# Router weights as the stationary operand, and both parts of the GLU's input as one moving operand

## The chip, the cores and the metric

The kernel runs on one core of a Trainium2 chip. A core has TensorE (matrix products into PSUM, a small accumulator memory of eight banks), VectorE, ScalarE, GpSimd and SyncE, which issues the loads. The metric is the time of the program on the device in microseconds, the median of several runs.

## The reference

One decoder layer on 256 tokens of width 2048, all in float32. What matters here:

```python
# state-space branch, u: (256, 1024)
z = gelu(y)
out = z * sigmoid(z @ w_glu)               # w_glu: 1024 x 1024, "the GLU"
merged = sigmoid(gate_ssm) * (out @ w_branch_ssm) + sigmoid(gate_att) * (y_att @ w_branch_att)
x = x + merged @ w_out
# experts
h2 = rms_norm(x, ffn_norm_g)
g_logits = h2 @ router_group_w + router_group_b      # 4 groups
e_logits = h2 @ router_expert_w + router_expert_b    # 32 experts
# top group, top 2 of its 8 experts, gates; then for every expert e
x = x + combine[:, e] * ((silu(h2 @ w_gate[e]) * (h2 @ w_up[e])) @ w_down[e])
```

The 36 router columns (4 + 32) are one weight matrix of 2048 x 36 in the kernel.

## The kernel before

The first phase is a list of blocks of dense products, worked off in steps; each step takes a slab of 256 x 512 weights. A slab is loaded into `raw` five steps ahead and split two steps ahead into a high part `wh` (ScalarE) and a low part `wl` (VectorE) in a rounded float32 form that TensorE multiplies in one pass. The activations are kept as high and low parts too, and a product is the sum of three: high by high, low by high, high by low. Most blocks (`b_orient`) use the activations as the stationary operand and 512 weight columns as the moving one, with two PSUM tiles. The two GLU blocks (`a_orient`) use the weights as the stationary operand and 256 tokens of z as the moving one, with four PSUM tiles `acc` (there are four such banks, handed out in turn). `glu_fin` empties them: ScalarE takes the sigmoid out of PSUM, VectorE multiplies by z, and after all four ScalarE and VectorE split the result into `ys`, the input of the next block (`wbs`).

The last block is `wout`, in four quarters n. After each, x is transposed (`x2_tr`) and `route_mm` adds its share to the router's logits: the transposed x (128 x 128) is the stationary operand and 36 router columns the moving one, plain float32, which TensorE takes as two instructions per product. So there are four visits of 16 instructions. The last quarter's follow when the products are over. Then TensorE does 36 transposes without use (`keep_busy(WARM[0])`) while VectorE works out the norm `rs2`, adds the bias and selects group and experts (`first_max`, tiles R). A product with a triangular matrix (`ult`) gives each token its rank, and expert 0 begins: `gather` picks tokens, `gate_up` multiplies by the weights, four column groups at a time (`tile_position`).

In the second phase the weights of 32 experts stream through a ring of 11 buffers (10 later) of 2 MB, six pieces an expert; `load_piece` issues a piece's load when a buffer's products have been issued, and the load waits on the last of them. The first 7 pieces are loaded ahead, during the blocks before, the others as memory of the first phase comes free.

Every engine works off its instructions in the order in which the program writes them (a manual schedule); a helper records most of them, so that the profile shows line 77 for all.

Of the kernel before, what the change touches and what calls it, by code (L numbers as in the profile page):

```python
# [9 lines left out]
F32 = mybir.dt.float32  # L10
F32R = mybir.dt.float32r
I32 = mybir.dt.int32
AF = mybir.ActivationFunctionType
OP = mybir.AluOpType
# [3 lines left out]
P = 128  # L18
T = 256
# [63 lines left out]
def hybrid_block(ctx, tc, A, out):  # L83
    nc = tc.nc
    load = {"vec": 0.0, "act": 0.0, "pe": 0.0}
    vec = Meter(nc.vector, load, "vec")
    act = Meter(nc.scalar, load, "act")
    pe = Meter(nc.tensor, load, "pe")
    sp, pool = nc.sync, nc.gpsimd
# [3 lines left out]
    def unit(i, shape, dt, name):  # L93
        return U[i].tile(shape, dt, name=name, tag="u")
# [4 lines left out]
    cp = ctx.enter_context(tc.tile_pool(name="cp", bufs=1))  # L99
    wctx = ExitStack()  # L100
    cq = wctx.enter_context(tc.tile_pool(name="cq", bufs=1))
# [6 lines left out]
    def acc_tile(name="acc"):  # L108
        return pacc.tile([P, 512], F32, name=name, tag="acc")

    def bg_tile(k):
        return pbg.tile([P, 512], F32, name="bg" + "ab"[k], tag="bg" + "ab"[k])
# [4 lines left out]
    def add_block(src, nk, begin, mm, fin):  # L117
        blocks.append((src, nk, begin, mm, fin))
# [12 lines left out]
    def split(i):  # L131
        if i >= len(subs):
# [12 lines left out]
    g1 = cq.tile([P, 16], F32, name="g1")  # L145

    small = cq.tile([P, 3, 32], F32, name="lamdt")
    cq.tile([P, 88], F32, name="level")
    dsk = cq.tile([P, 16], F32, name="dsk")
    qkg = cq.tile([P, 2], F32, name="qkg")  # L150
    g2 = cp.tile([P, 16], F32, name="g2")
    wrg = cq.tile([P, 16, 36], F32, name="wrg")
    rbias = cp.tile([P, 36], F32, name="rbias")
# [9 lines left out]
                       base=0, channel_multiplier=1)  # L163
    ult = cp.tile([P, P], F32, name="ult")
    pool.affine_select(out=ult, in_=ones, pattern=[[1, P]], compare_op=OP.is_gt, fill=0.0,
                       base=0, channel_multiplier=-1)
# [3 lines left out]
                       base=0, channel_multiplier=-1)  # L170
    dmask = cq.tile([P, 32], F32, name="dmask")
    pool.memset(dmask, 0.0)
    for i in range(4):
        pool.affine_select(out=dmask, in_=dmask, pattern=[[-1, 32]], compare_op=OP.not_equal, fill=1.0,
                           base=-32 * i, channel_multiplier=1)
# [22 lines left out]
    uT = uy[:, 0]  # L198
# [21 lines left out]

        add_block(src, nk, begin, mm, lambda: fin(st["a"]))

    def a_orient(src, nk, rh, rl, fin, banks, flag=None):
        st = {}

        def begin():
            if flag:
                need(flag)
            st["a"] = banks()

        def mm(s, h, l):
            for x, w in ((rh, h), (rl, h), (rh, l)):
                for kk in range(2):
                    k = 2 * s + kk
                    for m in range(4):
                        pe.matmul(st["a"][m][:, 0:T], w[:, kk, m * P:m * P + P], x(k),
                                  start=(k == 0 and w is h and x is rh), stop=(k == nk - 1 and w is l))

        add_block(src, nk, begin, mm, lambda: fin(st["a"]))

    acc4 = lambda: [acc_tile() for _ in range(4)]
# [27 lines left out]
    S = {}  # L269
# [47 lines left out]
    def glu_fin(n):  # L317
        def f(a):
            if n == 0:
                ys = unit(7, [P, 2, 8, T], F32R, "ys")  # L320
                S["ys"] = (ys[:, 0], ys[:, 1])
            for m in range(4):
                b = 4 * n + m
                act.activation(uT[:, b], a[m][:, 0:T], AF.Sigmoid)
                vec.tensor_tensor(uT[:, b], uT[:, b], yT[:, b], op=OP.mult)
            for m in range(0, 4, 2):
                b = slice(4 * n + m, 4 * n + m + 2)
                act.copy(S["ys"][0][:, b], uT[:, b])
                vec.tensor_tensor(S["ys"][1][:, b], uT[:, b], S["ys"][0][:, b], op=OP.subtract)
        return f  # L330

    for n in range(2):
        a_orient(A["wglu"][n], 8, lambda k: S["z"][0][:, k], lambda k: S["z"][1][:, k], glu_fin(n), acc4, "z")

    def ssm_fin(n):
        def f(a):
# [25 lines left out]
        b_orient(A["wbs"][n], 8, lambda k: S["ys"][0][:, k], lambda k: S["ys"][1][:, k], ssm_fin(n))  # L362

    ssq = cp.tile([P, 2, 4], F32, name="ssq")
    def out_fin(n):
        def f(a):
            c = slice(512 * n, 512 * n + 512)
            x2 = S["x2"]
            if n == 0:
                S["xt2"] = {}  # L370
                S["lg"] = [bg_tile(1), bg_tile(1)]
            for t in range(2):
                vec.tensor_tensor(x2[:, t, c], x2[:, t, c], a[t], op=OP.add)
            for t in range(2):
                later(D_X2 if n < 3 else 1, lambda t=t: x2_tr(n, t))
            for t in range(2):
                later(D_ROUTE if n < 3 else 2, lambda t=t: route_mm(n, t))
        return f

    def x2_tr(n, t):  # L380
        ps = bg_tile(0)
        for i in range(4):
            k = 4 * n + i
            pe.transpose(ps[:, P * i:P * i + P], S["x2"][:, t, P * k:P * k + P], ident)
        xt = S["xt2"][n, t] = slot((2 * n + t) % 4, [P, 4, P], F32, "xt2")
        act.copy(xt, ps.rearrange("p (i c) -> p i c", i=4))
        junk = slot(4 + (2 * n + t) % 4, [P, 512], F32, "junk")
        xs = S["x2"][:, t, 512 * n:512 * n + 512]
        if n < 3:
            act.activation(junk, xs, AF.Square, accum_out=ssq[:, t, n:n + 1])  # L390
            if n == 2 and t == 1:
                act.activation(tiny, ones[:, 0:1], AF.Sqrt)
        else:
            vec.scalar_tensor_tensor(junk, xs, 1.0, xs, op0=OP.mult, op1=OP.mult, accum_out=ssq[:, t, n:n + 1])

    def route_mm(n, t):
        for i in range(4):
            k = 4 * n + i
            pe.matmul(S["lg"][t][:, 0:36], S["xt2"][n, t][:, i], wrg[:, k], start=(k == 0), stop=(k == 15))

    for n in range(4):
        b_orient(A["wout"][n], 16, lambda k: S["m"][k // 8][:, 0, k % 8], lambda k: S["m"][k // 8][:, 1, k % 8], out_fin(n))
# [4 lines left out]
    for b, s in turns:  # L407
        src, nk, begin, mm, fin = blocks[b]
# [318 lines left out]
    def gelu():  # L727
        while "scan" not in prog:
            yield 0
        while "att" not in prog:  # L730
            yield 0
        zz = unit(9, [P, 2, 8, T], F32R, "zz")
        S["z"] = (zz[:, 0], zz[:, 1])
        c0 = math.sqrt(2.0 / math.pi) * 0.044715
        stage = [0] * 4
        while min(stage) < 5:
            for p in range(4):
                y, w = yT[:, 2 * p:2 * p + 2], uT[:, 2 * p:2 * p + 2]
                k = stage[p]
                if k > 4 or ("y", 2 * p + 1) not in prog:  # L740
                    continue
                if k == 0:
                    act.activation(w, y, AF.Square)
                elif k == 1:
                    vec.scalar_tensor_tensor(w, w, 1.0 / 0.044715, y, op0=OP.add, op1=OP.mult)
                elif k == 2:
                    act.activation(w, w, AF.Tanh, scale=c0)
                    vec.tensor_scalar(y, y, 0.5, None, op0=OP.mult)
                elif k == 3:
                    vec.scalar_tensor_tensor(y, w, 1.0, y, op0=OP.add, op1=OP.mult)  # L750
                    act.copy(S["z"][0][:, 2 * p:2 * p + 2], y)
                else:
                    vec.tensor_tensor(S["z"][1][:, 2 * p:2 * p + 2], y, S["z"][0][:, 2 * p:2 * p + 2], op=OP.subtract)
                stage[p] += 1
            yield 0
        prog["z"] = True
# [125 lines left out]
    def later(d, f):  # L882
        pend.append((prog["step"] + d, f))
# [9 lines left out]
    def need(flag):  # L893
        while flag not in prog:
            assert gens
            for g in list(gens):
                if next(g, None) is None:
                    gens.remove(g)
# [8 lines left out]
    for i in range(nsub):  # L907
        prog["step"] = i
        src, s, nk, begin, mm, fin = subs[i]
# [8 lines left out]
        h, l = hl_t.pop(i)  # L918
# [35 lines left out]
    rt = ctx.enter_context(tc.tile_pool(name="rt", bufs=1, reuse_waits="tile"))  # L954
# [4 lines left out]
    def keep_busy(n):  # L959
        ps = acc_tile()  # L960
        for _ in range(n):
            pe.transpose(ps[:, 0:P], ident, ident)

    keep_busy(WARM[0])
    r2 = cp.tile([P, 4, 2], F32, name="r2")
    vec.tensor_reduce(r2[:, 0], ssq, axis=AX.X, op=OP.add)
    vec.tensor_scalar(r2[:, 1], r2[:, 0], 1.0 / D, EPS, op0=OP.mult, op1=OP.add)
    rsqrt(r2[:, 2], r2[:, 1], r2[:, 3])
    rs2 = r2[:, 2]
    lg = rt.tile([P, 2, 36], F32, name="lgs")  # L970
    for t in range(2):
        vec.scalar_tensor_tensor(lg[:, t], S["lg"][t][:, 0:36], rs2[:, t:t + 1], rbias, op0=OP.mult, op1=OP.add)
    R1 = rt.tile([P, 2, 2], F32, name="R1")
    R4 = rt.tile([P, 9, 2, 4], F32, name="R4")
    R32 = rt.tile([P, 6, 2, 4, 8], F32, name="R32")
# [211 lines left out]
    with tc.For_i(0, novr) as it:  # L1187
        er = nc.values_load(oli[0:1, bass.ds(it + 1, 1)], min_val=0, max_val=NE - 1)
        gp = [acc_tile() for _ in range(4)]
        for k4 in range(4):  # L1190
            sp.dma_start(WO[k4], A["wgu"][bass.ds(er, 1), :, 4 * k4:4 * k4 + 4, :].rearrange("a p k c -> p (a k) c"))
            for t in range(2):
                ps = bg_tile(0)
                for i in range(4):
                    k = 4 * k4 + i
# [3 lines left out]
            for i in range(4):  # L1199
                k = 4 * k4 + i  # L1200
                for t in range(2):
                    for hf in range(2):
                        pe.matmul(gp[2 * t + hf], XO[:, k, P * t:P * t + P], WO[k4][:, i, 512 * hf:512 * hf + 512],
                                  start=(k == 0), stop=(k == 15))
# [12 lines left out]
        for t in range(2):  # L1217
            for n in range(4):
                ps = acc_tile()
                for j in range(4):  # L1220
                    pe.matmul(ps, hOT[:, j, P * t:P * t + P], WO[n // 2][:, j, 512 * (n % 2):512 * (n % 2) + 512],
                              start=(j == 0), stop=(j == 3))
                c = slice(512 * n, 512 * n + 512)
                vec.scalar_tensor_tensor(accv[:, t, c], ps, Go[:, t, bass.ds(er, 1)], accv[:, t, c],
                                         op0=OP.mult, op1=OP.add)
# [54 lines left out]
```

## Time and profile before

| what | value |
|---|---|
| median of 3 runs | 1563.29 us (1561.04 to 1563.48) |
| the profiled execution | 1564.15 us |
| its span in the trace | 1562.4 us |
| TensorE busy | 1263.4 us (81%) |
| VectorE busy | 541.0 us (35%) |
| ScalarE busy | 451.4 us (29%) |
| GpSimd busy | 55.9 us (4%) |
| read from device memory | 513.14 MB |

Busy times count an instruction from its start to its modelled end; shares are of the span. The span runs from the first to the last instruction; the time of an execution holds some 2 us around it.

### The profile page before, as it was taken

The numbers are of one execution on the slowest core, as the hardware profiler recorded it, in microseconds if no ns is written. First come the engines' busy times: TensorE is split into PE (matmuls) and PEld (weight loads), VectorE is DVE, ScalarE is ACT, GpSimd is POOL, SyncE is SP. The second block draws the span as 40 slices with busy tenths as digits, with TensorE's granted clock in tenths as the row PEclk, the third lists the DMA queues.
The fourth block names the chain that finished last, engine by engine and source line by source line (L and its number), as shares of the span: only waits on it lengthen the run. The fifth ranks groups of instructions, "written<-read, shape, count | busy, mean of one in ns | idle before, by whom it ended". The sixth has DMA issues, their size and how long they took to land.

```text
span 1562.4 us, 25151 instructions
## 1 busy us (share of the span) xinstructions
PE 1263.4 (81%) x10662; PEld 862.0 (55%) x10662; DVE 541.0 (35%) x1338; ACT 451.4 (29%) x768; POOL 55.9 (4%) x111
## 2 busy tenths in 40 slices
PE   9999999999999999987558557657657657657697
PEld 7878888888879888644224224323324323323364
DVE  7746878898856744302002002002002002001001
ACT  5645567554455444120100100110110110110101
POOL 6700000000000000000000000000000000000000
PEclk9999999999999999999879878878988779878899
DMA  8545655566657886999999999999999999999996
GB/s 266 175 131 159 195 153 158 163 193 189 202 191 256 277 281 229 379 427 427 427 427 428 428 426 426 428 428 427 427 427 427 426 428 428 426 428 427 426 426 242
DMA packets 65108, 516.91 MB, mean 331 GB/s; under 512 B 7905, under 2 KB 8161, under 8 KB 41441
## 3 DMA queue, kind: packets, MB, share of 16 engines
q1 hardware_dynamic: 64704, 515.21, 83.9%
q8 instruction: 86, 1.41, 0.4%
q14 instruction: 30, 0.24, 0.0%
q10 hardware_dynamic: 288, 0.06, 0.0%
HBM read 513.14 MB, written 2.10 MB: 330 GB/s over the span
## 4 chain that ended last, share of the span: by engine, by line
DMA 53%; PE 43%; DVE 2%; ACT 1%; issue 1%; SPq 0%; DVEq 0%
PE acc L77 38%; DMA ew<-wgu 33%; DMA ew<-wd 19%; PE bga L77 3%; PE bgb L77 2%; DVE wl L77 1%; ACT XY L77 0%; DMA raw<-win 0%; DVE R L77 0%; ACT wh L77 0%; DVE BC L77 0%; DVE Vs L77 0%; ACT AT L77 0%; ACT uy L77 0%; DVE prod L77 0%
## 5 line engine op out<-in xcount | busy, mean ns | idle before, releaser
L77 PE MATMUL acc<-ew,XY 128*32 128x256 f32 x4096 | 306.1, 451 | 159.3 <-DMA ew<-wgu 159.1
L77 PEld LDWEIGHTS acc<-ew,XY 128*32 128x32 f32 x4096 | 140.8, 125 | 308.1 <-DMA ew<-wgu 175.0
L77 DVE TENSOR_TENSOR wl<-raw,wh 128x1024 fp32r<-128x1024 f32 (+1 forms) x201 | 244.9, 1222 | 146.9 <-ACT wh L77 145.8
L77 ACT CAST wh<-raw 128x1024 fp32r<-128x1024 f32 x199 | 208.5, 1052 | 180.0 <-PE acc L77 121.3
L77 DVE TENSOR_TENSOR sg<-sg,acc 128x128 f32<-128x128 f32 x32 | 9.2, 288 | 642.3 <-ACT sg L77 642.3
L77 PE MATMUL acc<-ew,hT 128*32 128x256 f32 (+1 forms) x2080 | 155.0, 450 | 76.7 <-DMA ew<-wd 46.1
L77 ACT COPY XY<-acc 32x256 f32<-32x256 f32 (+1 forms) x260 | 93.7, 360 | 224.7 <-PE acc L77 222.2
L77 PEld LDWEIGHTS acc<-ew,hT 128*32 128x32 f32 x2080 | 76.5, 126 | 144.8 <-issue 69.8
L77 PE MATMUL acc<-wh,xh 128*128 128x512 f32 x512 | 145.6, 401 | 1.6 <-ACT wh L77 0.9
L77 PE MATMUL acc<-wh,xl 128*128 128x512 f32 x512 | 140.8, 392 | 0.0
L77 PE MATMUL acc<-wl,xh 128*128 128x512 f32 x512 | 140.4, 391 | 0.0
L77 ACT ACTIVATE sg<-acc 128x128 f32<-128x128 f32 x32 | 8.9, 278 | 402.0 <-PE acc L77 402.0
L77 PEld LDWEIGHTS acc<-wh,xl 128*128 128x128 f32 x512 | 97.0, 189 | 21.0
L77 PEld LDWEIGHTS acc<-wl,xh 128*128 128x128 f32 x512 | 96.7, 189 | 20.5
L77 PEld LDWEIGHTS acc<-wh,xh 128*128 128x128 f32 x512 | 93.9, 190 | 21.1 <-ACT wh L77 1.9
L77 PE MATMUL acc<-XY,sc 128*128 128x512 f32 x128 | 66.4, 663 | 14.5 <-ACT XY L77 14.5
L77 DVE TENSOR_TENSOR Vs<-Vs,prod 128x32 f32<-128x32 f32 x508 | 76.7, 221 | 0.0
L77 DVE TENSOR_TENSOR accv<-accv,acc 128x512 f32<-128x512 f32 x56 | 38.5, 687 | 97.6 <-PE acc L77 97.6
L77 PE MATMUL bga<-SL,x 128*128 128x128 f32 x512 | 63.5, 280 | 10.3 <-DVE SL L77 10.3
L77 PEld LDWEIGHTS bga<-SL,x 128*128 128x128 f32 x512 | 59.0, 192 | 22.9 <-DVE SL L77 15.8
L77 PE MATMUL acc<-wh,m 128*128 128x512 f32 x256 | 64.6, 392 | 0.0
L77 DVE TENSOR_TENSOR prod<-Vs,coef 128x64 f32<-128x64 f32 x254 | 56.0, 262 | 0.0
(222 smaller groups left out, 984.1 us busy)
## 6 DMA issues: line engine op xcount, KB each, us to landing
ew<-wgu SPq DMA_DIRECT2D x123, 2048.0 KB, 39.1
ew<-wd SPq DMA_DIRECT2D x61, 2048.0 KB, 39.1
raw<-win SPq DMA_DIRECT2D x127, 512.0 KB, 4.1
raw<-wout SPq DMA_DIRECT2D x32, 512.0 KB, 4.5
ew<-wgu SPq DMA_DIRECT2D x20, 512.0 KB, 6.2
raw<-wba SPq DMA_DIRECT2D x16, 512.0 KB, 4.6
raw<-wbs SPq DMA_DIRECT2D x16, 512.0 KB, 5.3
raw<-wglu SPq DMA_DIRECT2D x8, 512.0 KB, 4.9
```

The costliest lines, as they stand in the source:

```text
L77: return f(out, *args, **kw)
```

## The change

The router's weights become the stationary operand (36 columns loaded) and the transposed x the moving one (128 columns). Even and odd slices of the 2048 go to two column groups of TensorE and add up in PSUM rows 0 to 35 and 64 to 99. After the last visit ScalarE copies both into `lgT`, and a matmul of `lgT` with `sel`, which has ones at the two places of each column, adds the halves and turns the logits back to tokens by columns.

In the GLU the high and the low part of z lie side by side (`zz` is slice by part by token), so that one product of 512 columns stands where two of 256 stood; the low half collects in the upper half of the bank. `glu_fin` copies the upper half out, adds the lower, takes the sigmoid from SBUF and multiplies as before. "level" is an unused tile that pads the memory.

```diff
--- before.py
+++ after.py
@@ -145,7 +145,7 @@
     g1 = cq.tile([P, 16], F32, name="g1")
 
     small = cq.tile([P, 3, 32], F32, name="lamdt")
-    cq.tile([P, 88], F32, name="level")
+    cq.tile([P, 48], F32, name="level")
     dsk = cq.tile([P, 16], F32, name="dsk")
     qkg = cq.tile([P, 2], F32, name="qkg")
     g2 = cp.tile([P, 16], F32, name="g2")
@@ -220,7 +220,7 @@
 
         add_block(src, nk, begin, mm, lambda: fin(st["a"]))
 
-    def a_orient(src, nk, rh, rl, fin, banks, flag=None):
+    def a_orient(src, nk, rhl, rh, fin, banks, flag=None):
         st = {}
 
         def begin():
@@ -229,12 +229,12 @@
             st["a"] = banks()
 
         def mm(s, h, l):
-            for x, w in ((rh, h), (rl, h), (rh, l)):
+            for x, w, n in ((rhl, h, 2 * T), (rh, l, T)):
                 for kk in range(2):
                     k = 2 * s + kk
                     for m in range(4):
-                        pe.matmul(st["a"][m][:, 0:T], w[:, kk, m * P:m * P + P], x(k),
-                                  start=(k == 0 and w is h and x is rh), stop=(k == nk - 1 and w is l))
+                        pe.matmul(st["a"][m][:, 0:n], w[:, kk, m * P:m * P + P], x(k), start=(k == 0 and w is h),
+                                  stop=(k == nk - 1 and w is l))
 
         add_block(src, nk, begin, mm, lambda: fin(st["a"]))
 
@@ -321,7 +321,9 @@
                 S["ys"] = (ys[:, 0], ys[:, 1])
             for m in range(4):
                 b = 4 * n + m
-                act.activation(uT[:, b], a[m][:, 0:T], AF.Sigmoid)
+                vec.tensor_copy(uT[:, b], a[m][:, T:2 * T])
+                vec.tensor_tensor(uT[:, b], uT[:, b], a[m][:, 0:T], op=OP.add)
+                act.activation(uT[:, b], uT[:, b], AF.Sigmoid)
                 vec.tensor_tensor(uT[:, b], uT[:, b], yT[:, b], op=OP.mult)
             for m in range(0, 4, 2):
                 b = slice(4 * n + m, 4 * n + m + 2)
@@ -330,7 +332,7 @@
         return f
 
     for n in range(2):
-        a_orient(A["wglu"][n], 8, lambda k: S["z"][0][:, k], lambda k: S["z"][1][:, k], glu_fin(n), acc4, "z")
+        a_orient(A["wglu"][n], 8, lambda k: S["zz"][:, k].rearrange("p a t -> p (a t)"), lambda k: S["zz"][:, k, 0], glu_fin(n), acc4, "z")
 
     def ssm_fin(n):
         def f(a):
@@ -362,6 +364,11 @@
         b_orient(A["wbs"][n], 8, lambda k: S["ys"][0][:, k], lambda k: S["ys"][1][:, k], ssm_fin(n))
 
     ssq = cp.tile([P, 2, 4], F32, name="ssq")
+    sel = cp.tile([P, 36], F32, name="sel")
+    pool.memset(sel, 0.0)
+    for r in (0, 64):
+        pool.affine_select(out=sel, in_=sel, pattern=[[-1, 36]], compare_op=OP.not_equal, fill=1.0, base=-r,
+                           channel_multiplier=1)
     def out_fin(n):
         def f(a):
             c = slice(512 * n, 512 * n + 512)
@@ -396,7 +403,9 @@
     def route_mm(n, t):
         for i in range(4):
             k = 4 * n + i
-            pe.matmul(S["lg"][t][:, 0:36], S["xt2"][n, t][:, i], wrg[:, k], start=(k == 0), stop=(k == 15))
+            r = 64 * (k % 2)
+            pe.matmul(S["lg"][t][r:r + 36, 0:P], wrg[:, k], S["xt2"][n, t][:, i], start=(k < 2), stop=(k > 13),
+                      tile_position=(0, r))
 
     for n in range(4):
         b_orient(A["wout"][n], 16, lambda k: S["m"][k // 8][:, 0, k % 8], lambda k: S["m"][k // 8][:, 1, k % 8], out_fin(n))
@@ -729,8 +738,9 @@
             yield 0
         while "att" not in prog:
             yield 0
-        zz = unit(9, [P, 2, 8, T], F32R, "zz")
-        S["z"] = (zz[:, 0], zz[:, 1])
+        zz = unit(9, [P, 8, 2, T], F32R, "zz")
+        S["zz"] = zz
+        S["z"] = (zz[:, :, 0], zz[:, :, 1])
         c0 = math.sqrt(2.0 / math.pi) * 0.044715
         stage = [0] * 4
         while min(stage) < 5:
@@ -962,14 +972,21 @@
             pe.transpose(ps[:, 0:P], ident, ident)
 
     keep_busy(WARM[0])
+    lgT = rt.tile([P, T], F32, name="lgT")
+    vec.memset(lgT, 0.0)
+    for r in (0, 64):
+        for t in range(2):
+            act.copy(lgT[r:r + 36, P * t:P * t + P], S["lg"][t][r:r + 36, 0:P])
     r2 = cp.tile([P, 4, 2], F32, name="r2")
     vec.tensor_reduce(r2[:, 0], ssq, axis=AX.X, op=OP.add)
     vec.tensor_scalar(r2[:, 1], r2[:, 0], 1.0 / D, EPS, op0=OP.mult, op1=OP.add)
     rsqrt(r2[:, 2], r2[:, 1], r2[:, 3])
     rs2 = r2[:, 2]
     lg = rt.tile([P, 2, 36], F32, name="lgs")
+    lps = bg_tile(1)
     for t in range(2):
-        vec.scalar_tensor_tensor(lg[:, t], S["lg"][t][:, 0:36], rs2[:, t:t + 1], rbias, op0=OP.mult, op1=OP.add)
+        pe.matmul(lps[:, 64 * t:64 * t + 36], lgT[:, P * t:P * t + P], sel, start=True, stop=True)
+        vec.scalar_tensor_tensor(lg[:, t], lps[:, 64 * t:64 * t + 36], rs2[:, t:t + 1], rbias, op0=OP.mult, op1=OP.add)
     R1 = rt.tile([P, 2, 2], F32, name="R1")
     R4 = rt.tile([P, 9, 2, 4], F32, name="R4")
     R32 = rt.tile([P, 6, 2, 4, 8], F32, name="R32")
```

## Rows read from the trace of the kernel before

**Rows 1.** Stretches: span, busy us (instructions) per engine, PEclk, DMA share, GB/s.

```profile
505.00:635.00 130.00, 129.66 (x630) 108.73 (x628) 69.58 (x73) 55.47 (x71) 0.00 (x0) 1.00 0.78 268
...
700.00:1420.00 720.00, 470.11 (x5207) 237.22 (x5203) 63.38 (x120) 85.09 (x246) 0.00 (x0) 0.84 1.01 427
```

**Rows 2.** The same view, one microsecond at the seam.

```profile
646.00:647.00 1.00, 1.00 (x19) 0.52 (x8) 0.00 (x0) 0.00 (x0) 0.00 (x0) 1.00 0.08 33
```

**Rows 3.** SyncE's queue: start, us to the last one's end, what, count.

```profile
636.74 10.33 SPq L873 DMA_DIRECT2D ew<-wd  x2
...
652.38 14.58 SPq L873 DMA_DIRECT2D ew<-wgu  x4
```

**Rows 4.** Timeline of all engines at the seam: start, us, engine, operation.

```profile
644.75 1.93 PE L77 MATMUL acc<-ew,XY 128*32 128x256 f32 x32
```

**Rows 5.** Timeline around the finish of the first GLU block.

```profile
472.41 2.08 PE L77 MATMUL acc<-zz,wh 128*128 128x256 f32 x16
...
478.01 1.21 ACT L77 ACTIVATE uy<-acc 128x256 f32<-128x256 f32 x4 [2.43 <-PE acc L77]
...
478.43 1.43 DVE L77 TENSOR_TENSOR uy<-uy 128x256 f32<-128x256 f32 x4 [1.59 <-ACT uy L77]
...
478.45 2.65 PE L77 MATMUL acc<-zz,wh 128*128 128x256 f32 x16
```

**Rows 6.** Groups by form: busy us, mean ns | idle before, releaser.

```profile
L77 DVE TENSOR_TENSOR ya<-bgb,ya 128x256 fp32r<-128x256 f32 x8 | 3.4, 423 | 5.1 <-ACT ya L77 5.1
...
L77 DVE TENSOR_SCALAR uy<-uy 128x512 f32<-128x512 f32 x4 | 1.7, 422 | 0.0
...
L77 ACT ACTIVATE uy<-acc 128x256 f32<-128x256 f32 x8 | 2.4, 390 | 2.7 <-PE acc L77 2.7
...
L77 ACT ACTIVATE uy<-uy 128x512 f32<-128x512 f32 x8 | 4.8, 630 | 0.0
...
L77 ACT CAST ys<-uy 128x512 fp32r<-128x512 f32 x4 | 2.5, 622 | 0.6 <-DVE uy L77 0.5
...
L77 ACT CAST wh<-raw 128x1024 fp32r<-128x1024 f32 x199 | 208.5, 1052 | 180.0 <-PE acc L77 121.3 <-DMA raw<-win 19.5 <-DMA raw<-wbs 8.3
```

**Rows 7.** Chain of work around a route visit: start, us, what, count.

```profile
566.34 2.73 PE acc L77 x12
...
569.08 1.71 PE bgb L77 x16
```

**Rows 8.** Timeline of TensorE, first and last of 13 starts on two row groups.

```profile
102.25 0.27 PE L77 MATMUL bga<-uy,BT 64*128 64x128 f32 x1
...
102.92 0.27 PE L77 MATMUL bgb<-uy,BT 64*128 64x128 f32 x1
```

**Rows 9.** Chain of work between two visits in column groups.

```profile
95.02 2.98 PE acc L77 x12
```

**Rows 10.** Timeline of the last route products and the routing.

```profile
634.74 1.92 PE L77 MATMUL bgb<-wrg,xt 128*128 128x36 f32 x16
...
636.49 4.13 PE L77 MATMUL acc<-ident 128*128 128x128 f32 x36
...
637.15 0.42 DVE L77 SCALAR_TENSOR_TENSOR lgs<-bgb,r,rbias 128x36 f32<-128x36 f32 x2
...
637.60 0.29 DVE L77 TENSOR_REDUCE R<-lgs 128x8 f32<-128x64 f32 x2
...
640.98 0.43 PE L77 MATMUL bgb<-R,ult 128*128 128x64 f32 x2 [0.36 <-DVE R L77]
```

**Rows 11.** Stretches of one microsecond around a fall of the granted clock.

```profile
705.00:706.00 1.00, 0.00 (x0) 0.00 (x0) 0.00 (x0) 0.00 (x0) 0.00 (x0) 1.00 1.06 442
...
708.00:709.00 1.00, 0.93 (x12) 0.05 (x4) 0.00 (x0) 0.03 (x1) 0.00 (x0) 0.50 1.08 459
...
714.00:715.00 1.00, 0.77 (x12) 0.12 (x4) 0.00 (x0) 0.17 (x1) 0.00 (x0) 0.80 1.12 475
```

**Rows 12.** Timeline of GpSimd: its wait before the state-space constants.

```profile
12.28 1.03 POOL L549 TENSOR_SCALAR sm<-lamdt 128x32 f32<-128x32 f32 x1 [8.53 <-DMA lamdt<-lamdt]
```

## Prediction, made before the change was run

> **What bounds the kernel now.** I read first the table of engines and DMA by stretches. Up to 635 us TensorE is the limit: it is busy 129.66 of the 130 us from 505 to 635, at the full clock. From 700 to 1420 us it is busy 470 of 720 us, while the DMA engines are busy throughout and move 427 GB/s [rows 1]. So there are two phases: dense products, bound by TensorE, then the experts, bound by the stream of their weights (192 pieces of 2 MB, of which 11 fit ahead).
>
> The seam decides what a delay is worth. In the microsecond from 646 to 647 the DMA engines are 0.08 busy [rows 2]: the eleven pieces have landed and no buffer is free. SyncE's queue shows what it waits for: a piece is issued at about 646.7 (the second of the two that begin at 636.74) and the next at 652.38 [rows 3]. These are the ends of the first two groups of 32 expert products (the first runs from 644.75 to 646.68) [rows 4]: each gives one ring buffer back. After that the stream does not stop. So every microsecond by which TensorE reaches expert 0 later, in the dense phase or in the routing, is a microsecond at the end, and every one saved there is one gained. Nothing is absorbed, since the stream is already dry at the seam.
>
> **GLU products.** A slab takes 24 matmuls of 256 columns now. Sixteen take 2.08 us with the last one's 0.28, so 0.12 each [rows 5] and 2.88 a slab. After: eight of 512 columns and eight of 256. Twelve of 512 columns take 2.73 us, 0.2275 each [rows 7]; the slab takes 8 x 0.2275 + 8 x 0.12 = 2.78. Eight slabs: -0.8 us. Two operands side by side save little, because the columns are the same.
>
> The finish of the block grows. Now, per bank, ScalarE reads the bank (sigmoid) and frees it; four take 1.21 us, the first 0.39, and TensorE starts the next block 0.05 us after the first (478.45 against 478.01 and 0.39) [rows 5, 6]. After, per bank, VectorE copies one half, adds the other, ScalarE takes the sigmoid, VectorE multiplies; and VectorE works in order, so the copy of bank m+1 stands behind the product of bank m, which waits for the sigmoid of m. Prices: add and product 0.42 each (128x256); the copy has no row: a 256-wide VectorE operation with a tensor from PSUM takes 0.42, half of a 512-wide scalar operation in SBUF is 0.21, and I take 0.35; the sigmoid from SBUF between 0.39 and 0.42 (0.63 for 512), 0.41 [rows 6]; two hand-overs of 0.04. That is 1.68 us per bank. The fourth bank comes free 3 x 1.68 + 0.77 = 5.8 us after the block's end, where it was 1.2 us. The next block's first four products go to the four banks in turn, so TensorE stands: +4.6 us (3.8 to 4.9 over the bounds).
>
> By the Trainium skill, "VectorE: DVE Perf Modes", section "Why PSUM operands drop a tier", a VectorE operation on fp32 from PSUM gets no faster mode; by that rule the copy costs 0.42 and the two finishes about 0.3 us more. No run here shows such a copy.
>
> At the second finish the next block (the SSM branch) needs two banks. The second is free 1.68 + 0.77 after the end, where it was 0.67 (0.39 and the 0.27 by which the sigmoids follow each other): +1.8 us. Behind it on ScalarE stand the four sigmoids, two casts of ys (0.62 each) and the next split's cast (1.05) [rows 6]. The last product ends 6.7 us after, the second cast 7.4, the split's cast 8.4; TensorE wants that slab at 7.7: +0.7 us. Together +2.5 (1.5 to 3.2). The same queue after the first finish costs nothing: TensorE comes to that slab only at 10 us. GLU: -0.8 + 4.6 + 2.5 = **+6.3 us** (4.5 to 7.3).
>
> **Router products, first three visits.** Sixteen matmuls take 1.71 us, 0.107 each [rows 7], though only 36 columns move: loading 128 columns sets the pace. After, 36 columns are loaded and 128 move, on two column groups. The nearest rows are two row groups of 128 columns: 13 starts in 0.67 us, 0.056 each [rows 8], so sixteen take 0.9. Changing the grouping costs: twelve full products between two grouped visits took 2.98 us, against 2.73 [rows 9, 7], 0.25 for going in and out. A visit goes from 1.71 to 1.15, and three give -1.7 us. Ends: a rate of four groups (half again) gives -3.0; no overlap at all gives +0.75.
>
> The Trainium skill, "TensorEngine Tiling (Array Packing)", section "Key Properties", says that changing the tiling mode drains TensorE, which speaks against four short visits. The trace agrees with 0.25 us a visit; without that the three would give -2.5 us.
>
> **Last visit and routing.** Now the last route products run from 634.74, then 36 warm-up transposes from 636.49 [rows 10]. VectorE needs nothing from TensorE after the route products: its two bias operations begin at 637.15 and the selection chain at 637.60, beside the warm-up. After, the logits must go through ScalarE (four copies of 36x128) and through TensorE once more, and that matmul is behind the warm-up in TensorE's queue. The copies are ready by about 637.5 and wait. The second half of the last visit still waits for its transposed x, so the warm-up begins only 0.35 us earlier, at 636.15. At (4.13 - 0.27) / 35 = 0.11 us each it ends at 640.1. The two selecting matmuls are four instructions, with their bias operations about 0.95 us more. The chain begins at 641.1 in place of 637.60: **+3.5 us** (3.3 if the second matmul overlaps the first bias operation fully, 4.0 if it waits for it). The memset, copies and the later square root lie under the warm-up; were that gone they would cost about 1 us.
>
> **The clock.** Both waits leave TensorE idle. It stood idle in 705 to 706 at a granted clock of 1.00; in 708 to 709, just after it had restarted, the grant was 0.50 (1.2 GHz), and it was coming back only in 714 to 715 [rows 11]. The same will follow the GLU wait (four products in 5.4 us) and the routing, where the warm-up is over at 641 and the next matmul, now at 640.98 beside its end [rows 10], comes 3.5 us later. At half clock TensorE's work takes twice as long. If it is busy through all of the six or so us, that loses 3; where it also waits, less. I take 1.6 for each fall (0 to 3.3): **+3.2 us**.
>
> **Hidden.** `sel` is made on GpSimd before its 8.53 us wait for a load, which ends at 12.28 [rows 12]; its three operations cost nothing, about 1 us on GpSimd without that gap. The new order of zz moves the same elements. The smaller "level" only makes room for `sel`.
>
> **Sum.** 6.3 - 1.7 + 3.5 + 3.2 = +11.3 us. The profiled execution took 1564.15 us, so 1575.4 there; that one lies 0.9 above the median, and on the median of 1563.29 it is **1574.6 us**.
>
> **Rivals.**
> 1. The waits come, the clock holds or falls only once: +8.1 to +9.7, 1571.4 to 1573. For it: the row is one unbroken pause, and the GLU's is broken by single products. Against: the idle 705 to 706, after which it fell.
> 2. The weight stream sets the end and takes the delays in. Place: the first two ring buffers given back. Time: no change, 1563.3. It decides if the stream still has ten us of pieces to land when expert 0's first group is done. For it: the stream is at 427 GB/s for the whole second phase. Against: the 0.08 in 646 to 647 [rows 2], where it is dry already, and every buffer's load is issued behind the same late TensorE.
> 3. The finish does not hold TensorE (the copies and adds run ahead of the products, so banks come free at 0.77 us each): the GLU costs about +2.0, the routing still 3.5, no fall in the GLU: +5.4, 1568.7. Against: in the finish of now VectorE's four products follow ScalarE's sigmoids in the program's order [rows 5].
> 4. The edits do what they save and nothing waits: -0.8 - 1.7 - 0.35 = -2.9, 1560.4. It would need the selecting matmul to overtake the warm-up; no row shows a matmul that overtakes another without a change of group.
>
> **How the numbers follow.** Forecast 0.55, rival 1 0.24, rival 2 0.06, rival 3 0.09, rival 4 0.06. What a measurement of this kernel can tell from no change is 0.2%, 3.1 us. Faster: 0.05 (rival 4, whose gain lies just inside it, with a better column rate); within 0.2%: 0.07; slower: 0.88. The low end is the waits at their lower bounds without a fall: 4.5 - 3.0 + 3.3 = +4.8, 1568.1, and a little below for rival 3: 1567. The high end is 7.3 + 0 + 4.0 + 4.5 = +15.8: 1579.
>
> **What would show it.** In the profile after: the first product on the fourth GLU bank some 5.5 us after the block's last; VectorE in the order copy, add, product with waits for ScalarE; route visits of about 0.9 us for 16; the selecting matmuls right after the warm-up's last transpose; the gap in the stream at the seam about 5 us wider than now; a grant of 0.50 after the GLU finish and after the routing. I am wrong if TensorE runs on through the GLU finish, if the route products take 1.7 us as before, or if the stream shows no wider gap at the seam.

## The result and the profile after

| | before | after |
|---|---|---|
| median | 1563.38 us (4 runs) | 1578.47 us (4 runs, 1577.24 to 1579.39) |
| ratio | | 1.0097, 95% interval [1.0084, 1.0111] |
| profiled execution | 1564.15 us | 1577.63 us |
| its span | 1562.4 us | 1575.8 us |

The change costs 15.1 us by the medians and 13.5 by the two profiled executions. The traces explain the 13.5; the rest is between executions of one kernel, and stays open. Forecast were +11.3 us, 1574.6, in a range of 1567 to 1579. Two executions in the series below ran far longer (2426.49 us of the kernel before, 4930.71 us of e2_merge_late) and are left out of every time.

**The stretches**, in the view of [rows 1]: the experts' phase is as it was, so the whole loss lies ahead of it.

```profile
505.00:635.00 130.00, 128.69 (x627) 105.72 (x626) 73.33 (x76) 58.05 (x73) 0.00 (x0) 1.00 0.79 266
700.00:1420.00 720.00, 470.44 (x5249) 238.35 (x5245) 63.72 (x121) 88.30 (x256) 0.00 (x0) 0.84 1.01 427
```

**The first GLU finish.** The timeline of all engines that answers to [rows 5]; in brackets stand the idle time of the engine before the line and what ended it:

```profile
477.86 0.42 DVE L77 COPY uy<-acc 128x256 f32<-128x256 f32 x1 [1.08 <-PE acc L77]
478.32 0.42 DVE L77 TENSOR_TENSOR uy<-uy,acc 128x256 f32<-128x256 f32 x1
478.77 0.42 ACT L77 ACTIVATE uy<-uy 128x256 f32<-128x256 f32 x1 [3.25 <-DVE uy L77]
478.88 0.47 PE L77 MATMUL acc<-zz,wh 128*128 128x512 f32 x1 [0.71 <-DVE uy L77]
479.22 0.43 DVE L77 TENSOR_TENSOR uy<-uy 128x256 f32<-128x256 f32 x1 [0.48 <-ACT uy L77]
479.56 0.42 DVE L77 COPY uy<-acc 128x256 f32<-128x256 f32 x1
...
480.58 0.47 PE L77 MATMUL acc<-zz,wh 128*128 128x512 f32 x1 [1.23 <-DVE uy L77]
...
483.97 2.47 PE L77 MATMUL acc<-zz,wh 128*128 128x512 f32 x5 [1.23 <-DVE uy L77]
```

Read it as a circle. VectorE copies and adds, hands over to ScalarE, waits 0.48 us for the sigmoid, multiplies, and only then copies the next bank at 479.56. TensorE starts once per turn: 478.88, 480.58, and at 483.97 on the fourth bank, a pitch of 1.70 us. The windows, in the columns of [rows 1], show what follows. The granted clock is 0.50 (1.2 GHz) just after the last of these waits, which makes a mean of 0.62 over 484 to 488. After the second finish the DMA engines stand still:

```profile
484.00:488.00 4.00, 4.00 (x15) 3.47 (x16) 3.12 (x5) 3.38 (x5) 0.00 (x0) 0.62 0.07 29
485.00:486.00 1.00, 1.00 (x4) 0.81 (x3) 1.00 (x2) 1.00 (x2) 0.00 (x0) 0.50 0.04 16
...
500.00:505.00 5.00, 4.66 (x21) 3.57 (x20) 3.66 (x8) 3.62 (x6) 0.00 (x0) 1.00 0.00 0
```

**The block behind it (wbs).** This was in no step of the forecast; the timeline, with SyncE's queue first:

```profile
494.74 11.15 SPq L129 DMA_DIRECT2D raw<-wbs  x2
...
504.31 3.50 DVE L77 TENSOR_TENSOR wl<-raw,wh 128x1024 fp32r<-128x1024 f32 x3 [0.26 <-ACT wh L77]
...
509.76 1.05 ACT L77 CAST wh<-raw 128x1024 fp32r<-128x1024 f32 x1 [3.58 <-DMA raw<-wbs]
510.84 1.23 DVE L77 TENSOR_TENSOR wl<-raw,wh 128x1024 fp32r<-128x1024 f32 x1 [3.03 <-ACT wh L77]
511.98 0.69 DVE L77 TENSOR_TENSOR gate<-acc,gate 128x512 f32<-128x512 f32 x1
...
513.45 0.66 PE L77 MATMUL bga<-ident,gate 128*128 128x128 f32 x4 [0.65 <-DVE gate L77]
...
514.77 0.66 PE L77 MATMUL bgb<-ident,gate 128*128 128x128 f32 x4 [0.67 <-DVE gate L77]
```

Follow the releasers upward. The merge transposes wait for the gate products, which stand on VectorE behind the low part of a slab. VectorE waited 3.03 us for the high part, and that cast 3.58 us for a load. The load came late because VectorE, held up by the finish, gave the `raw` buffers back late: it forms the low part of three slabs only from 504.31 on, and the second of the two loads that begin at 494.74, ended at 505.89, had waited 10.4 us for that. Before, these transposes stood without idle time (TensorE's timeline):

```profile
504.59 0.60 PE L77 MATMUL bga<-ident,gate 128*128 128x128 f32 x4
505.02 0.60 PE L77 MATMUL bgb<-ident,gate 128*128 128x128 f32 x4
```

**Route visits and the seam.** TensorE's timeline, for [rows 7] and [rows 10]: one early visit, then the last visit and the routing.

```profile
578.84 1.07 PE L77 MATMUL bgb<-xt,wrg 128*36 128x128 f32 x16
...
643.00 1.38 PE L77 MATMUL bgb<-xt,wrg 128*36 128x128 f32 x16
644.31 4.15 PE L77 MATMUL acc<-ident 128*128 128x128 f32 x36
648.30 0.31 PE L77 MATMUL bgb<-sel,lgT 128*128 128x36 f32 x2
649.05 0.38 PE L77 MATMUL bgb<-sel,lgT 128*128 128x36 f32 x2 [0.44 <-DVE lgs L77]
653.13 0.69 PE L77 MATMUL bgb<-R,ult 128*128 128x64 f32 x2 [3.70 <-DVE R L77]
...
658.58 1.93 PE L77 MATMUL acc<-ew,XY 128*32 128x256 f32 x32
```

VectorE's timeline has the first reduction of the chain at 649.76, against 637.60 [rows 10]:

```profile
649.76 0.29 DVE L77 TENSOR_REDUCE R<-lgs 128x8 f32<-128x64 f32 x2
```

The seam in the windows (as [rows 2]), half clock and then a dry stream; and SyncE's queue (as [rows 3]), the piece that was issued at 652.38:

```profile
650.00:658.00 8.00, 4.87 (x24) 4.87 (x25) 4.49 (x26) 0.42 (x2) 0.00 (x0) 0.57 0.58 246
...
658.00:659.00 1.00, 1.00 (x14) 0.74 (x17) 0.43 (x2) 0.00 (x0) 0.00 (x0) 1.00 0.00 0
```

```profile
666.21 0.33 SPq L883 DMA_DIRECT2D ew<-wgu  x1
```

Expert 0 starts 13.83 us later, the piece is issued 13.83 later, and the span is 13.4 longer. The gap in the stream is wider too: by the windows of one microsecond the DMA engines are idle for 6.4 us in 654 to 661, where it was 1.9 us in 645 to 649.

### The profile page after: what moved, and what is told of

It reads as the page before. It is cut to its first block, busy times and chain, and to the rows that moved or that the text cites. A ratio compares the mean times of both kernels' runs of the same rounds, so it can differ in the third digit from the quotient of the medians.

```text
span 1575.8 us, 25065 instructions
## 1 busy us (share of the span) xinstructions
PE 1261.6 (80%) x10602; PEld 855.6 (54%) x10602; DVE 548.1 (35%) x1355; ACT 452.0 (29%) x772; POOL 56.7 (4%) x114
## 5 line engine op out<-in xcount | busy, mean ns | idle before, releaser
L77 PE MATMUL acc<-ew,XY 128*32 128x256 f32 x4096 | 312.5, 459 | 168.1 <-DMA ew<-wgu 168.0
L77 PE MATMUL acc<-ew,hT 128*32 128x256 f32 (+1 forms) x2080 | 149.4, 437 | 71.0 <-DMA ew<-wd 37.7
L77 PE MATMUL acc<-XY,sc 128*128 128x512 f32 x128 | 61.7, 622 | 14.6 <-ACT XY L77 14.5
```

What stands on the lines that cost most here:

```text
L77: return f(out, *args, **kw)
```

## The experiments

Each ratio is to the kernel before on the same chip (medians of 1563.6 to 1563.8); "from after" is the difference to 1578.47. The changed kernel was not run again beside them, so a difference from after of one or two microseconds is not clear of noise by itself, and the traces are needed for it. Diffs are shown in part, and are to the changed kernel unless said otherwise.

**1 and 2. Each half alone.** e1_glu_only puts `a_orient`, `glu_fin` and `zz` of the change into the kernel before; e1_router_only takes these three back out of the changed kernel. Of the first, `glu_fin`, against the kernel before:

```diff
-                act.activation(uT[:, b], a[m][:, 0:T], AF.Sigmoid)
+                vec.tensor_copy(uT[:, b], a[m][:, T:2 * T])
+                vec.tensor_tensor(uT[:, b], uT[:, b], a[m][:, 0:T], op=OP.add)
+                act.activation(uT[:, b], uT[:, b], AF.Sigmoid)
```

> The kernel before with the GLU edits alone (products of 512 columns, the longer finish, the new order of zz); the router as before. Theory (waits behind the longer finish): about 9.7 us above before, 1573: the two finishes hold TensorE for 4.9 and 2.2 us, the clock falls once, 1.5, the first merge transposes wait 1.7 for VectorE. Rival (the terms of the prediction only, nothing queued behind the second finish): 7.9 us, 1571. If the router's edits carry most of the loss, under 4 us.

> The kernel before with the router edits alone; the GLU as before. Theory: three visits save 0.55 each, -1.7; routing chain later by 4.0 behind the warm-up; clock falls once in the routing, +1.7: about 4.0 us above before, 1567.4. Rival (the two edits are not additive, the stream takes part of the delay in): the sum of this and the GLU alone differs from 13.5 by more than 2 us. Rival (the select step costs nothing): 1.7 us below before.

Measured: GLU alone 1574.45 us, 1.0072 [1.0054, 1.0089], +10.8; router alone 1567.29, 1.0025 [1.0015, 1.0035], +3.7. Together 14.5 of the 15.1, so the halves add up: both stand ahead of the same dry seam. The router is as expected; the GLU costs 1.1 more. In its profile the clock falls a second time (see the last section).

**3. Free all four banks first (e1_banks_first).** The products move into a loop of their own behind the copies, additions and sigmoids.

```diff
                 act.activation(uT[:, b], uT[:, b], AF.Sigmoid)
+            for m in range(4):
+                b = 4 * n + m
                 vec.tensor_tensor(uT[:, b], uT[:, b], yT[:, b], op=OP.mult)
```

> The changed kernel, but in the GLU finish VectorE does copy and add of all four banks before the four products. Theory (banks are freed too late because the next copy stands behind a product that waits for ScalarE): banks come free every 0.9 us and not every 1.7; the fourth 2.5 us earlier, in the second finish the second 0.8 earlier, no clock fall in the GLU (1.5), and less waiting behind it: 5 to 7 us below the changed kernel, 1572. Rival (the number of VectorE operations on the path is what costs, not their order): within 1 us of the changed kernel.

Measured: 1572.40 us, 1.0050 [1.0033, 1.0067], 6.1 below after. TensorE's timeline:

```profile
478.52 0.47 PE L77 MATMUL acc<-zz,wh 128*128 128x512 f32 x1 [0.71 <-DVE uy L77]
479.31 0.47 PE L77 MATMUL acc<-zz,wh 128*128 128x512 f32 x1 [0.32 <-DVE uy L77]
...
480.89 1.40 PE L77 MATMUL acc<-zz,wh 128*128 128x512 f32 x5 [0.32 <-DVE uy L77]
...
507.94 0.66 PE L77 MATMUL bgb<-ident,gate 128*128 128x128 f32 x4 [0.67 <-DVE gate L77]
```

The pitch falls from 1.70 to 0.79 us, and the granted clock is 1.00 in every window from 470 to 516. So the order on VectorE is the cause of most of the loss. The added operations cost some even so: the table behind experiment 9 has 61.66 us for this kernel, 58.74 for the one before and 68.14 for after. One merge transpose still waits.

**4. Select ahead of the warm-up (e1_select_first).**

```diff
-    keep_busy(WARM[0])
...
     for t in range(2):
         pe.matmul(lps[:, 64 * t:64 * t + 36], lgT[:, P * t:P * t + P], sel, start=True, stop=True)
+    keep_busy(WARM[0])
+    for t in range(2):
         vec.scalar_tensor_tensor(lg[:, t], lps[:, 64 * t:64 * t + 36], rs2[:, t:t + 1], rbias, op0=OP.mult, op1=OP.add)
```

> The changed kernel with the 36 warm-up transposes after the two selecting matmuls and not before them. Theory (the select waits in TensorE's queue behind the warm-up): the selection chain begins 2.4 us earlier, bound by memset, copies and square root, and TensorE is busy beside it, so that the clock doesn't fall: 4.1 us below the changed kernel, 1574.4. Rival (the copies through ScalarE and the square root behind them are the cost): within 1 us of the changed kernel. Rival (the clock falls all the same): 2.4 below.

Measured: 1574.11 us, 1.0064 [1.0048, 1.0081], -4.4 from after. TensorE's timeline, and the window of the routing:

```profile
645.30 0.64 PE L77 MATMUL bgb<-sel,lgT 128*128 128x36 f32 x4 [1.18 <-ACT lgT L77]
645.77 4.13 PE L77 MATMUL acc<-ident 128*128 128x128 f32 x36
...
654.36 1.93 PE L77 MATMUL acc<-ew,XY 128*32 128x256 f32 x32
```

```profile
650.00:656.00 6.00, 5.14 (x60) 4.10 (x60) 2.59 (x11) 0.21 (x1) 0.00 (x0) 1.00 0.67 287
```

Expert 0 starts 4.2 us earlier (3.96 of it behind the last route visit) and the clock stays up: the two selecting matmuls did stand behind the 36 transposes. What remains is 1.18 us in which TensorE waits for ScalarE's copies.

**5. Keep the clock in the routing (e2_warm_on).** 28 more transposes of the identity behind the bias operations.

```diff
+    keep_busy(28)
     R1 = rt.tile([P, 2, 2], F32, name="R1")
```

> The changed kernel with 28 more warm-up transposes after the selecting matmuls, beside the selection chain. Theory (the clock falls because TensorE is idle beside the chain, and costs 1.7 us until expert 0's first products): the grant stays at 1.00 and the time is 1.7 us below the changed kernel, 1576.8. Rival (the fall costs nothing at the end, as the stream makes it up): within 0.5 us of the changed kernel.

Measured: 1576.75 us, 1.0087 [1.0072, 1.0103], -1.7 from after. The window, where after had 0.57 over 650 to 658:

```profile
650.00:656.00 6.00, 5.10 (x45) 4.66 (x44) 4.07 (x23) 0.42 (x2) 0.00 (x0) 1.00 0.72 306
```

The intervals of this kernel and of after overlap, but the traces agree with the time: from the second selecting matmul to expert 0 it is 9.53 us in after (649.05 to 658.58) and 7.86 here (648.68 to 656.54). The clock's fall in the routing cost those 1.7.

**6. Merge transposes one slab later (e2_merge_late).** First test of the missed term. `D_MERGE` is the number of steps by which these transposes are put off.

```diff
-D_MERGE = 1
+D_MERGE = 2
```

> The changed kernel with the transposes of the merged branches one step later (D_MERGE 2 in place of 1). Theory (1.7 us of the GLU's cost are the first two merge transposes, which wait for VectorE's gate products behind a split whose slab was loaded late): they find their operands ready, 1.7 us below the changed kernel, 1576.8. Rival (the wait only shows there, and TensorE waits elsewhere in its place): within 0.5 us of the changed kernel.

Measured: 1578.69 us, 1.0097 [1.0079, 1.0116]: no gain, as the rival has it. The trace doesn't bear the rival out, though. The transposes no longer wait (517.42 and 517.85, without idle time), but the clock fell longer, where after had 0.62 and then 1.00:

```profile
484.00:488.00 4.00, 4.00 (x14) 3.47 (x14) 3.01 (x5) 3.05 (x4) 0.00 (x0) 0.50 0.01 4
488.00:490.00 2.00, 2.00 (x6) 1.54 (x5) 1.14 (x1) 0.00 (x0) 0.00 (x0) 0.54 0.71 168
```

Half clock also came back, with 0.51 over 500 to 502. Up to the merge transposes the program is that of after, so the edit isn't what lengthened the fall; e1_glu_only and e2_warm_on, which have the GLU of after, had such falls as well (last section). Two causes moved against each other, and the time could not tell them apart. So the clock had to be held first.

**7 to 9. The same with the clock held.** e3_glu_warm gives TensorE transposes of the identity where it waits for banks: 6, 10, 10 and 10 ahead of the first products of the second GLU block, 6 and 10 ahead of those on wbs. e3_glu_warm_merge is that with `D_MERGE = 2`, and e3_banks_merge is number 3 with `D_MERGE = 2`.

```diff
+                        if fills and k == 0 and w is h and x is rhl:
+                            fill(fills[m])
                         pe.matmul(st["a"][m][:, 0:n], w[:, kk, m * P:m * P + P], x(k), start=(k == 0 and w is h),
...
+                            if fills and k == 0 and w is h and x is lh:
+                                fill(fills[t])
```

> The changed kernel with TensorE given transposes of the identity (6, 10, 10 and 10) ahead of the first products on the four banks of the second gate block, and 6 and 10 ahead of the first two of the block on wbs, where it waits for VectorE in the changed kernel. Theory: the pitch of the banks stays 1.70 us, but the granted clock stays at 1.00 through 480:505, so the second gate block gets back the 1.6 us that it ran at half clock; the merge transposes still wait about 1.3 us for the gate products: 1576.9 us. Rival: what the block on wbs waits for is the chain of slabs alone, and the clock's 1.6 us come back as a longer wait there: 1578.4 us.

> The kernel with the filled waits (e3_glu_warm) and the merge transposes one slab later (D_MERGE 2). Theory: with the clock held, moving the transposes behind the next slab takes their wait of some 0.9 to 1.7 us out of the time, where it could not show in the run without the fills, because the clock fell longer: 1575.5 us, 1.4 below e3_glu_warm. Rival: the wait is for the late slab itself, whatever stands behind it, and the two kernels agree within 0.4 us.

> Copies and additions of all four banks ahead of the products (e1_banks_first, 1572.40 us, where no clock fell) and D_MERGE 2. Theory: the first products on m start 0.8 to 1.0 us earlier than in e1_banks_first (at 539.3 us of the span instead of 540.18), and the time is 1571.5 us. Rival: 540.2 and 1572.4 us.

Measured: 1576.63 us, 1.0086 [1.0072, 1.0100]; 1574.47, 1.0071 [1.0057, 1.0085]; 1570.27, 1.0037 [1.0023, 1.0050]. The intervals of the first two overlap, that of the first and of after too, so the traces decide. In e3_glu_warm the pitch is unchanged, with the fills in the waits (TensorE's timeline), and the clock holds (window):

```profile
477.17 0.47 PE L77 MATMUL acc<-zz,wh 128*128 128x512 f32 x1
477.48 1.25 PE L77 MATMUL bga<-ident 128*128 128x128 f32 x10
478.87 0.47 PE L77 MATMUL acc<-zz,wh 128*128 128x512 f32 x1
```

```profile
484.00:488.00 4.00, 4.00 (x25) 3.54 (x24) 3.21 (x4) 2.64 (x3) 0.00 (x0) 1.00 0.26 41
```

One measure compares all of them: the time from the first product of the second GLU block to the first product of `wout` on m.

| kernel | from, to (us) | takes |
|---|---|---|
| before | 478.45, 537.19 | 58.74 |
| after | 478.88, 547.02 | 68.14 |
| e3_glu_warm | 477.17, 543.72 | 66.55 |
| e3_glu_warm_merge | 481.50, 546.39 | 64.89 |
| e1_banks_first | 478.52, 540.18 | 61.66 |
| e3_banks_merge | 478.48, 539.25 | 60.77 |

Each row is one execution. They reach the block at different times (e3_glu_warm_merge 4.3 us behind e3_glu_warm), which the measure takes out. The clock is worth 1.59 us against the execution of after, the wait of the merge transposes 1.66 with the fills and 0.89 with the banks first. The rivals (no gain from the clock, no gain from the later transposes) fall. In time, e3_banks_merge came out 1.2 us below its forecast and e3_glu_warm_merge 1.0; their intervals are some 4 us wide.

**10 and 11. Both halves mended.** e2_route_best is the router edit alone with its causes taken away: GpSimd clears lgT ahead, ScalarE does the copies and TensorE the selection before a warm-up of 30, and the first two visits are done as one. e2_both_mended adds the GLU edit with banks first and `D_MERGE = 2`. The first, against the kernel before:

```diff
+    lgT = slot(4, [P, T], F32, "lgT")
+    pool.memset(lgT, 0.0)
...
+    for t in range(2):
+        for r in (0, 64):
+            act.copy(lgT[r:r + 36, P * t:P * t + P], S["lg"][t][r:r + 36, 0:P])
+    for t in range(2):
+        pe.matmul(lps[:, 64 * t:64 * t + 36], lgT[:, P * t:P * t + P], sel, start=True, stop=True)
...
+    keep_busy(30)
...
-                later(D_ROUTE if n < 3 else 2, lambda t=t: route_mm(n, t))
+                later((D_ROUTE + (8 if n == 0 else 0)) if n < 3 else 2, lambda t=t: route_mm(n, t))
```

> The kernel before with the router edits alone, mended: lgT cleared ahead by GpSimd in other memory, the norm's operations before the copies, the selecting matmuls before the warm-up, which is cut to 30 transposes, and the first two route visits made one. Theory (visits in column groups save 0.55 us each, and the select step costs nothing when its copies lie under the norm's chain): three visits and one change of grouping saved, 1.9 us below the kernel before, 1561.7. Rival (the select step lies on the path whatever its order): 1 to 2 us above the kernel before.

> The mended router edits together with the GLU edits, these with copies and adds of all four banks first and the merge transposes one step later. Theory (even so the finish frees the fourth bank 3.3 us after the block's end and not 1.25, and the second bank 1.1 later in the second finish, against 0.8 saved in products): 2.4 us above the mended router alone, 1564.1. Rival (with its waits mended the GLU edit gains its 0.8): 0.8 below the mended router alone.

Measured: 1562.20 us, 0.9992 [0.9983, 1.0001], and 1564.04, 1.0008 [0.9999, 1.0017]. TensorE's timeline of e2_route_best:

```profile
634.73 0.87 PE L77 MATMUL bgb<-sel,lgT 128*128 128x36 f32 x4 [0.40 <-ACT lgT L77]
635.44 3.47 PE L77 MATMUL acc<-ident 128*128 128x128 f32 x30
...
643.25 1.93 PE L77 MATMUL acc<-ew,XY 128*32 128x256 f32 x32
```

Expert 0 starts 1.5 us earlier than before (644.75 in [rows 4]) and the median is 1.6 lower, about what the visits save (1.9 was forecast), but the interval still touches no change. The GLU edit loses some 1.8 us even so, where 2.4 were forecast and the rival had a gain of 0.8. The measure of the table agrees: 60.71 us in e2_both_mended (478.67 to 539.38), 58.76 in e2_route_best (478.61 to 537.37).

## Why the prediction was right, and where it was off

The forecast of slower, through waits of TensorE ahead of a dry seam, held. Step by step, by the shift of the same instructions between the two profiled traces:

| step | forecast | measured |
|---|---|---|
| GLU slabs | -0.10 a slab | pitch 2.79 for 2.88: -0.09 |
| pitch of the banks | 1.68 | 1.70 |
| first finish, its fall of the clock, slabs so far | +4.6 + 1.6 - 0.4 | +5.5 |
| second finish | +1.8, then +0.7 | about +2.0, then +0.65 |
| merge transposes on wbs | none | +1.74 |
| GLU in all, with its fall of the clock | +7.9 | +9.6 |
| three visits | -1.7 | -1.65 (9.81 to 8.16) |
| warm-up starts earlier | -0.35 | -0.34 (8.16 to 7.82) |
| selection | +3.5 | +4.0 (8.16 to 12.16) |
| clock in the routing | +1.6 | +1.7 (12.16 to 13.83) |
| span | +11.3 | +13.4 |

In the GLU the shift is 0.17 us already at the first product (466.56 to 466.73), which is taken off the first finish and the GLU in all; it is 5.68 us at the second slab of the second block (481.89 to 487.57), about 7.4 at the second product on wbs (498.51), 8.06 at the first slab of the second block there (501.86 to 509.92) and 9.80 behind the merge transposes (505.38 to 515.18).

**Right.** The circle on VectorE, its pitch, the place of the selecting matmuls in TensorE's queue and both falls of the clock came as forecast. Experiment 3 took the circle away with its fall of the clock, experiment 4 the place of the matmuls with theirs, experiments 7 and 5 each fall alone, and the time followed. Rival 1 fell with the two falls in after. Rival 2 (the stream takes the delays in) fell with 13.83 us of 13.83 passed on to the piece's issue. Rival 4 fell with its condition: no matmul overtook the warm-up. Rival 3 would have needed copies that run ahead of the products. Experiment 3 made that order, for which the forecast's terms give 5.9 us back (+2.0 in place of 6.3 and 1.6); it gave 6.1. Both ends lay higher than those terms, though: the table has +2.9 for this GLU and +9.4 for that of after.

**Luck.** That the clock would fall in both places was reasoned, but the 1.6 for each was picked between 0 and 3.3, so that 1.59 and 1.67 came out is luck in size. The range held barely: two of the four executions (1579.30 and 1579.39) lie above 1579, and its upper end was not the sum of all upper bounds (it has 0 for the visits, where the bound was +0.75, and 4.5 for the two falls, where it was 6.6).

**The step that was missed.** "The same queue after the first finish costs nothing" was checked for the slab's high part only, and the second finish was followed to one slab. The delay went on: later splits, later `raw` buffers, later loads, a late slab, and behind it on VectorE the gate products that the merge transposes need. That is the +1.74, most of the 2.1 us by which the sum fell short. That it hangs on the place of the transposes is shown by experiments 8 and 9. That a fourth `raw` buffer would cure it at the root was not tried.

**Mis-sized.** The selection came out at its upper bound, 4.0. The second matmul waits 0.44 us for the first bias operation [<-DVE lgs at 649.05], since both halves share one PSUM tile and the program writes matmul, bias, matmul, bias; in experiment 4, which writes both matmuls first, the four instructions follow each other in 0.64 us. The copy takes 0.42 us, not the 0.35 that was put between two rows. The Trainium skill, "VectorE: DVE Perf Modes", section "Why PSUM operands drop a tier", says that a PSUM operand keeps an fp32 operation of VectorE at the normal rate. The prediction's sentence on it gave 0.42, and here the trace agrees.

**Switching groups.** A visit of 16 changed the time by -0.55 us, against the -0.56 that the 0.25 us for going in and out left. By the Trainium skill, "TensorEngine Tiling (Array Packing)", section "Key Properties", a change of mode drains TensorE; the runs fit a price of that size, but none measured the drain alone. The nearest is e2_route_best, where the double visit of 32 instructions takes 1.94 us against 2 x 1.07 for two single ones.

## What to carry to other kernels

When an operand moves from one engine's read of PSUM to several engines in turn, write out the in-order queue of each engine and ask when every bank comes free, not how long the added operations take: here the order of the same instructions was worth 6 us. Put a matmul that a chain waits for ahead of any work that only keeps TensorE busy. And follow a delay until some buffer has slack: its next victim may be a load whose buffer comes back late, two blocks on.

## What the runs showed of the hardware that was not expected

The fall to half clock (1.2 GHz) was not of one length, though the instructions ahead of it were the same: five profiled executions have the first GLU finish of after, with the same broken wait. The granted clock by stretches, and the time from the first product of the second GLU block to the first product of `wout` on m, as in the table above:

| kernel | 480 to 484 | 484 to 488 | 488 to 490 | 500 to 502 | takes (us) |
|---|---|---|---|---|---|
| after | 0.96 | 0.62 | 1.00 | 1.00 | 68.14 |
| e1_select_first | 0.92 | 0.65 | 1.00 | 1.00 | 67.98 |
| e1_glu_only | 0.73 | 0.50 | 0.83 | 0.50 | 69.08 |
| e2_warm_on | 0.63 | 0.52 | 1.00 | 0.62 | 69.03 |
| e2_merge_late (`D_MERGE = 2`) | 0.87 | 0.50 | 0.54 | 0.51 | 68.76 |

Three of the five fell again after the second finish, as in e1_glu_only:

```profile
500.00:503.00 3.00, 3.00 (x10) 2.37 (x9) 1.98 (x5) 1.25 (x3) 0.00 (x0) 0.61 0.00 0
```

With the same GLU, the two executions that fell again (e1_glu_only, e2_warm_on) took some 1.0 us longer than the two that did not (after, e1_select_first), although their merge transposes waited less (0.47 and 0.57 us in place of two waits of about 0.6 each). So most of the 1.1 us that e1_glu_only costs more than forecast is there, and a time of one or two microseconds can come from where the clock falls in an execution. What makes one execution fall longer is not shown. Where the waits were filled (e3_glu_warm) or no longer than 0.7 us (e1_banks_first), the rows of the stretch show 1.00. Such a second fall could be part of the 1.6 us between the medians' difference and the profiled one; that was not tested.
